# Expert weights in longer rows, some of their lower parts on GpSimd, experts ordered by their count of tokens

## The chip, the core and the metric

One core of a Trainium2 chip runs the whole program. The metric is the device time of one execution in microseconds, lower is better.

## What is computed

The reference is a trunk of two layers. Each has a token mixer (an attention branch and a recurrent branch, merged) and a channel mixer: in the first layer a dense SwiGLU, in the second eight experts of which each token takes two. The change is in the experts alone.

```python
D_MODEL, SEQ, N_EXPERTS, TOP_K, D_FF_EXPERT = 1024, 256, 8, 2, 3584

def swiglu(t, w_gate, w_up, w_down):
    return (jax.nn.silu(t @ w_gate) * (t @ w_up)) @ w_down

def moe_swiglu(h, w_router, b_router, w_gate, w_up, w_down):
    t = h.reshape(B * S, D)
    logits = (t @ w_router).astype(F32) + b_router.astype(F32)
    top_val, top_idx = lax.top_k(logits, TOP_K)
    top_w = jax.nn.softmax(top_val, axis=-1)
    combine = jnp.sum(jax.nn.one_hot(top_idx, N_EXPERTS, dtype=F32) * top_w[..., None], axis=1)
    out = jnp.zeros((B * S, D), F32)
    for e in range(N_EXPERTS):
        out = out + combine[:, e:e + 1] * swiglu(t, w_gate[e], w_up[e], w_down[e]).astype(F32)
    return out.astype(h.dtype).reshape(B, S, D)
```

All data are float32.

## The kernel before

Every product is made of three: each operand is split into an upper part (rounded to the type that TensorE reads at one column a cycle, a copy on ScalarE, L93) and a lower part (the rest, a subtraction on VectorE, L97, by `lower`), and `mm3` (L113 to L115) adds upper x upper, upper x lower and lower x upper in PSUM.

The experts run one after the other, each for 128 slots, whatever its count of tokens; at 128 tokens or fewer the block behind `tc.If` at the end is not entered. `begin` gathers the rows of the first two experts by products with a one-hot matrix (`places_in` builds it, `taken` multiplies, L1271), and makes the first 512 hidden columns of the first expert. `run` then makes a list of parts. A part is 1 MB of weights: four row blocks of 512 columns of gate or up (`column_part`, rows of 2 KB in memory), or two row blocks of whole rows of down (`down_part`, 4 KB). One block of 512 hidden columns is four parts of gate and up, then two parts of down for the block before. `loads` issues the weights on SP's queue into a ring of 14 tiles of 8 KB a partition (`ORDER`, and four tiles once); a tile is free when its lower part is made.

For each part m the emitted order is: its 12 products, hooks of slot 0, the split of the first half of part m + 2 (`half`: ScalarE's copy L93 of 128x1024, then VectorE's L97), hooks of slot 1, the split of the second half, hooks of slot 2. Upper and lower parts have four tiles each (`NSP`), so a half is split when the products of the half four before it are done. Hooks are the small stages: `silu` (L1480, ScalarE from PSUM), `times_up` (L1483, VectorE, one input in PSUM), `turn_hidden` (four transposes, L308), `hidden_high` (L1496, ScalarE) and `hidden_low` (L1500, VectorE from PSUM), `gate_out` (L1504), `gated_high` (L1508) and `gated_low` (L1512, GpSimd), `scatter_in` (L1541) and `scatter_add` (L1545), and for the next pair of experts `places_in` (L1250), `gather_in`, `gather_rows` (L1526), `gather_high` (L1531) and `gather_low` (L1536, GpSimd). Pairs are experts (0,1), (2,3), (4,5), (6,7), gathered in the odd experts. `one_of` makes the second expert's rows of the first pair. The root of the norm is a power on GpSimd (L302).

GpSimd also works at the start of the kernel: `shift_sums` (L544, L548) multiplies and adds tiles there while VectorE splits the first weights (L97, L617).

Of the kernel before, what the change touches and what calls it, by code (L numbers as in the profile page):

```python
# [17 lines left out]
P = 128  # L18
D = 1024
KD = D // P  # L20
S = 256
# [19 lines left out]
def hybrid_trunk_kernel(  # L41
# [12 lines left out]
    pre = pre_stack.enter_context(tc.tile_pool(name="pre", bufs=1, reuse_waits="tile"))   # of the work before the experts  # L54
# [9 lines left out]
    wraw = (wp, "raw", NRAW)  # L64
    ring = [[wraw], 0, []]      # tiles in turn, how many were taken, tiles to take once after the first turn
# [32 lines left out]

    def pairs_of(w):
        return [(w[1][:, j], w[2][:, j]) for j in range(w[1].shape[1])]  # L100

    def piece(src, nk, n):
        """split weights, one (hi, lo) pair for each of the nk row blocks"""
        raw = load_raw(src, nk, n)
        r = []
        for k in range(0, nk, 2):
            w = halves(raw[:, k:k + 2])
            lower(*w)
            r += pairs_of(w)
        return r  # L110
# [7 lines left out]
    side = []      # [generator, steps for each piece, steps owed]  # L118
# [81 lines left out]
    # rows transposed to one column per 128 channels: gains of the four norms, lb rows of both layers, gains of q and k  # L200
    # (1 beyond their 64 channels); the same for b_ada
# [28 lines left out]
    rt = {}      # of the routing  # L230
# [9 lines left out]
    ada = const.tile([P, DEPTH, 4, KD], F32, name="ada")   # sh1, sc1, sh2, sc2 as columns; sc becomes gain*(1+sc)  # L240
# [70 lines left out]
    def affine(tp, dst, l, sc, sh, half):  # L311
        """dst = gain (1 + sc) xn + sh, channels on the partitions"""
# [12 lines left out]
    class HT:  # L325
        """transposed normed activations in two parts, [128 channels, 256 tokens] for each of the 8 channel blocks"""
# [59 lines left out]
    def proj(get, wsrc, col, n, banks=None):  # L386
        """token-major [128, n] PSUM banks of h @ w[:, col:col+n], one for each token tile"""
# [6 lines left out]
    def proj_t(hT, wsrc, col, n):  # L394
        """channel-major: banks of two [128 channels, 256 tokens] blocks of (h @ w[:, col:col+n])^T"""
# [109 lines left out]
    def start(pool, hT, win):  # L505
        """the first weights meet one or two blocks of channels at a time, as their adaLN vectors come in"""
# [24 lines left out]
        def sums(q):  # L531
            """partial sums of the scale over the rows that a partition holds"""
# [8 lines left out]
        def shift_sums(q):  # L541
            """those of the shift, in place"""
# [98 lines left out]
    def mixer(l, hT=None, first=None, half_first=None):  # L641
        with tc.tile_pool(name=f"mix{l}", bufs=1, reuse_waits="tile") as mp:
            win = w_in[l]
            if l:
                # in the order in which their last uses come, the last to be free first
# [16 lines left out]
            # lower bound of the forget gate: none in layer 0, softmax over the layers' rows in layer 1  # L662
# [71 lines left out]
            def hgrn(gi, lfh, lfl, kq, hv):  # L734
# [5 lines left out]
                for hp in range(2):  # L740
# [4 lines left out]
                    for i in range(NT):  # L745
                        e = mp.tile([P, 8, 2, P], F32, tag="ee", bufs=2, name="ee")
                        ee.append(e)
                        # decays to the middle of every block, on all levels, then the keys and queries under them
# [12 lines left out]
                        for li, m in enumerate(LV[:6]):  # L761
                            # keys in the left half of every block, queries in the right half
# [7 lines left out]
                        # pairs of tokens, from their first one on: the decay of the second one, on its query and off its key  # L770
# [6 lines left out]
                        # A^T[s, t]: the pairs of every level, the last of them with the diagonal  # L777
# [42 lines left out]
                # RMS norm over each head  # L820
# [9 lines left out]
            def fox_gate():  # L830
                # transposed: the 16 gate columns (and 16 beyond, unused) stationary, their upper parts beside their lower ones
# [165 lines left out]
    def router_rows(pool, l):  # L997
        """logits = x / rms(x) @ (gain (1 + sc) W) + (sh @ W + b): the weights and the row, before x is there"""
# [10 lines left out]
    def turn_rows(src, dst):  # L1009
        """four 128-channel blocks of x, transposed"""  # L1010
# [12 lines left out]
    def ranks(pool, i):  # L1023
        """the two experts of every token of tile i, as top_k orders them: larger logits first, equal ones by index"""
# [13 lines left out]
    def shares_in(pool):  # L1038
        """softmax over the two logits, in stages: the logits of the two"""
# [25 lines left out]
    def norm(i, hs=None):  # L1065
        """x / rms(x) in two parts"""
# [6 lines left out]
    def place(i, j):  # L1073
        """the places of the tokens of tile i among those of their experts: what the tokens of tile j add"""
# [140 lines left out]
    def moe(l, gate0):  # L1215
        with tc.tile_pool(name="moe", bufs=1, reuse_waits="tile") as mp:
            for tag, n, w in (("s01", 1, 32), ("pv", 1, 32), ("tv", 1, 8), ("ws", 1, 8), ("small", 1, SMALL), ("hid", 2, 512), ("hf", 1, 512), ("g", 3, 2048), ("th", 1, 512), ("tlo", 1, 512), ("ys", 1, 2048),
                              ("raw4", 1, 2048), ("raw8", 1, 2048), ("raw6", 1, 2048), ("raw5", 1, 2048), ("tm", 2, 8), ("ei", 1, 8), ("m8", 1, 8), ("cc", 8, 8), ("raw3", 2, 2048), ("raw2", 1, 2048), ("oneh", 1, 512), ("ohT", 2, 256), ("raw1", 2, 2048), ("raw7", 1, 2048)):
# [18 lines left out]
            # One expert for the slots first .. first+127 of its tokens, in stages: gather, columns of gate and up, rows of  # L1237
            # down, scatter. posc, selc, combc: [128, 1] columns for each token tile.
# [3 lines left out]
            def places_in(pair, i):  # L1242
                oneh = pair[0].get("oneh")
                if oneh is None:
                    oneh = mp.tile([P, NT, 2, P], F32R, tag="oneh", bufs=1, name="oneh")[:, :, :len(pair)]
                for n, ex in enumerate(pair):
                    ex["oneh"] = oneh
                    if ex["first"]:
                        v.tensor_scalar(out=ex["pos"][i], in0=ex["pos"][i], scalar1=float(-ex["first"]), scalar2=None, op0=OP.add)
                    (g if ex.get("e") else v).tensor_scalar(out=oneh[:, i, n], in0=iota, scalar1=ex["pos"][i], scalar2=ex["sel"][i], op0=OP.is_equal, op1=OP.mult)  # L1250
# [14 lines left out]
            def taken(pair, q, i, tp):  # L1265
                """channel blocks 2 q and 2 q + 1 of the tokens of both experts that are in tile i"""
# [39 lines left out]
            def hidden(ex, j):  # L1306
                t = mp.tile([P, 512], F32, tag="hid", bufs=2, name="hid")
# [17 lines left out]
            def gated(ex, h):  # L1325
                yg = mp.tile([P, 512], F32, tag="hid", bufs=2, name="yg")
# [17 lines left out]
            def an_expert(cl, first, w):  # L1344
                return dict(pos=cl[0], sel=cl[1], comb=cl[2], first=first, w=w)

            def begin(pair):
# [3 lines left out]
                xT = mp.tile([P, 512], F32, tag="hid", bufs=2, name="xT")  # L1351
# [30 lines left out]
                room = ["hf", "th", "tlo", "hid"]  # L1382
                hf = [mp.tile([P, 2, P], F32, tag=t, bufs=1 + (t == "hid"), name="hf0") for t in room]
# [41 lines left out]
                one_of(pair, 1, 0, tb[0])  # L1425
                pair[0]["b"] = bk
                pair[0]["tb"] = tb
# [359 lines left out]
```

## Time and profile before

| | |
|---|---|
| median of 3 runs | 1920.51 us (1918.06 to 1923.71) |
| span of the profiled execution | 1922.9 us |
| TensorE busy | 1855.0 us (96%) |
| VectorE busy | 1572.3 us (82%) |
| ScalarE busy | 1309.0 us (68%) |
| GpSimd busy | 212.3 us (11%) |
| read from HBM | 522.72 MB |

The profiled execution has a time of its own, its span; the median is of three executions without a profile. The experts run from about 930 us to the end. Busy time is a sum over stages with different limits, and a matmul's end is modelled: what an engine does in a stage is read from the stretches, the chain and the timeline of that stage.

### The profile page before, as it was taken

Reading aid. Unit: us, or ns where it says so; the run is one execution under the profiler, and the core shown is the slowest. Engines: PE = TensorE matmul, PEld = TensorE weight load, DVE = VectorE, ACT = ScalarE, POOL = GpSimd, SP = SyncE. Lnnn points to the kernel's source line nnn. Section 1 sums busy time; section 2 is a strip of 40 time slices with the busy share of each in tenths; the row PEclk is TensorE's granted clock in tenths of the full one; section 3 lists DMA queues with packets and bytes.
Section 4 is the critical chain, followed back from the end, with each engine's and each line's share of the span. In section 5 each row is a group of like instructions: output and inputs, shape, how many; then the busy total and the mean of one; then the engine's idle time right before and its main releaser. Section 6 shows DMA issues by size and latency. Waiting matters only on the chain.

```text
span 1922.9 us, 25537 instructions
## 1 busy us (share of the span) xinstructions
PE 1855.0 (96%) x9510; PEld 1539.4 (80%) x9510; DVE 1572.3 (82%) x2006; ACT 1309.0 (68%) x1664; POOL 212.3 (11%) x184
## 2 busy tenths in 40 slices
PE   2999999999999999999999999999999999999998
PEld 2787787889987878788787888888888888888887
DVE  6877865878867877447898989999899988999997
ACT  2466558554436665585788787787787878878775
POOL 6701200000000011100000210003100021000000
PEclk9898999999999989999999999999999999999999
DMA  9543653878864525338899999999999999999990
GB/s 300 181 141 110 222 187 118 306 280 308 302 249 134 182 83 174 111 110 306 304 346 355 347 340 370 365 374 343 350 362 362 374 350 340 375 356 368 357 366 26
DMA packets 235140, 525.50 MB, mean 273 GB/s; under 512 B 11756, under 2 KB 23292, under 8 KB 235008
## 3 DMA queue, kind: packets, MB, share of 16 engines
q1 hardware_dynamic: 233624, 523.61, 76.2%
q8 instruction: 76, 1.25, 0.3%
q14 instruction: 56, 0.46, 0.1%
q10 hardware_dynamic: 1384, 0.18, 0.1%
HBM read 522.72 MB, written 1.05 MB: 272 GB/s over the span
## 4 chain that ended last, share of the span: by engine, by line
PE 74%; DVE 2%; ACT 1%; issue 1%; POOL 1%; DVEq 0%; ACTq 0%; POOLq 0%
PE acc L115 15%; PE acc L114 15%; PE acc L113 15%; PE yb L114 5%; PE yb L115 5%; PE yb L113 5%; PE acc L412 2%; PE acc L411 2%; PE acc L413 2%; PE tb L308 2%; DVE wlo L97 1%; PE tb L1541 1%; POOL rs L302 1%; PE tb L798 1%; PE tb L1271 1%
## 5 line engine op out<-in xcount | busy, mean ns | idle before, releaser
L97 DVE TENSOR_TENSOR wlo<-raw,whi 128x1024 fp32r<-128x1024 f32 (+1 forms) x888 | 1077.0, 1237 | 140.6 <-ACT whi L93 123.9
L93 ACT CAST whi<-raw 128x1024 fp32r<-128x1024 f32 (+1 forms) x888 | 919.0, 1047 | 323.6 <-PE acc L115 195.9
L113 PE MATMUL acc<-whi,g 128*128 128x512 f32 x880 | 349.2, 397 | 0.0
L114 PE MATMUL acc<-wlo,g 128*128 128x512 f32 x880 | 344.2, 391 | 0.0
L115 PE MATMUL acc<-whi,g 128*128 128x512 f32 x880 | 344.2, 391 | 0.0
L114 PE MATMUL acc<-wlo,hTh 128*128 128x512 f32 x512 | 209.1, 409 | 6.5 <-DVE wlo L97 6.4
L113 PE MATMUL acc<-whi,hTh 128*128 128x512 f32 x512 | 212.1, 416 | 2.9 <-ACT hTh L615 2.4
L115 PE MATMUL acc<-whi,hTl 128*128 128x512 f32 x512 | 209.9, 410 | 2.6 <-DVE hTl L617 2.6
L114 PEld LDWEIGHTS acc<-wlo,g 128*128 128x128 f32 x880 | 165.5, 188 | 35.8 <-DVE wlo L97 2.8
L115 PEld LDWEIGHTS acc<-whi,g 128*128 128x128 f32 x880 | 165.1, 188 | 35.6
L113 PEld LDWEIGHTS acc<-whi,g 128*128 128x128 f32 x880 | 165.4, 188 | 32.8
L114 PE MATMUL yb<-wlo,th 128*128 128x512 f32 x440 | 172.5, 392 | 4.2 <-DVE wlo L97 4.2
L113 PE MATMUL yb<-whi,th 128*128 128x512 f32 x440 | 171.6, 390 | 0.0
L115 PE MATMUL yb<-whi,tlo 128*128 128x512 f32 x440 | 171.6, 390 | 0.0
L114 PEld LDWEIGHTS acc<-wlo,hTh 128*128 128x128 f32 x512 | 99.2, 194 | 27.8 <-DVE wlo L97 9.9
L115 PEld LDWEIGHTS acc<-whi,hTl 128*128 128x128 f32 x512 | 98.5, 192 | 23.8 <-DVE hTl L617 4.2
L411 PE MATMUL acc<-hTh,whi 128*128 128x256 f32 x416 | 117.2, 282 | 0.0
L412 PE MATMUL acc<-hTl,whi 128*128 128x256 f32 x416 | 116.4, 280 | 0.0
L413 PE MATMUL acc<-hTh,wlo 128*128 128x256 f32 x416 | 116.4, 280 | 0.0
L113 PEld LDWEIGHTS acc<-whi,hTh 128*128 128x128 f32 x512 | 98.2, 192 | 21.9 <-ACT hTh L615 3.1
L302 POOL TENSOR_TENSOR rs<-rs,mhalf 128x8 f32<-128x8 f32 (+1 forms) x28 | 50.9, 1818 | 540.0 <-DVE rs L301 507.8
L114 PEld LDWEIGHTS yb<-wlo,th 128*128 128x128 f32 x440 | 82.6, 188 | 25.9 <-DVE wlo L97 9.3
(382 smaller groups left out, 2645.1 us busy)
## 6 DMA issues: line engine op xcount, KB each, us to landing
raw<-in_moe_w_gate SPq DMA_DIRECT2D x112, 1024.0 KB, 6.0
raw<-in_moe_w_up SPq DMA_DIRECT2D x112, 1024.0 KB, 6.1
raw<-in_moe_w_down SPq DMA_DIRECT2D x110, 1024.0 KB, 5.7
raw<-in_w_in SPq DMA_DIRECT2D x66, 1024.0 KB, 5.1
raw<-in_w_ada SPq DMA_DIRECT2D x48, 1024.0 KB, 6.5
raw<-in_dense_w_gate SPq DMA_DIRECT2D x10, 1024.0 KB, 7.9
raw<-in_dense_w_up SPq DMA_DIRECT2D x10, 1024.0 KB, 7.3
raw<-in_dense_w_down SPq DMA_DIRECT2D x10, 1024.0 KB, 8.6
```

The lines of the kernel that those rows point to most:

```text
L93: a.copy(hi, raw)
L97: v.tensor_sub(lo, raw, hi.bitcast(F32))
L113: pe.matmul(out=o, lhsT=lh, rhs=rh, start=start, stop=False)
L114: pe.matmul(out=o, lhsT=lh, rhs=rl, start=False, stop=False)
L115: pe.matmul(out=o, lhsT=ll, rhs=rh, start=False, stop=stop)
L302: g.tensor_tensor(out=r, in0=r, in1=mhalf[:, :shape[1]], op=OP.pow)
L308: pe.transpose(out=tp[:, b * P:(b + 1) * P], in_=src(b), identity=ident)
L411: pe.matmul(out=o, lhsT=hi, rhs=hT.hh[:, k], start=(k == 0 and c % 2 == 0), stop=False)
L412: pe.matmul(out=o, lhsT=hi, rhs=hT.hl[:, k], start=False, stop=False)
L413: pe.matmul(out=o, lhsT=lo, rhs=hT.hh[:, k], start=False, stop=(k == KD - 1 and c % 2 == 1))
L798: pe.matmul(out=tv[:P - m, li, h, :].rearrange("p (b r) -> p b r", r=m), lhsT=el[:, :P - m], rhs=el.rearrange("p (b s r) -> p b s r", s=2, ...
L1271: pe.matmul(out=tp[:, b * 2 * P:(b * 2 + ne) * P], lhsT=src[:, i, kk * P:(kk + 1) * P], rhs=pair[0]["oneh"][:, i].rearrange("p n t -> p (n ...
```

## The change

- Blocks of hidden columns are 1024 wide (the first expert: 512, then three of 1024; the others: three of 1024, then 512). A part of gate or up is two row blocks of 1024 columns (4 KB rows); a part of down is two neighbouring rows for each partition (8 KB), for which the hidden columns are dealt to the transposes in that order (`PERM`, `view`).
- Of the lower parts, every sixth half (`POOLED`) is subtracted on GpSimd.
- Experts run in an order that is computed: expert 0 first, the others by their rank in the count of tokens (`TURNS`); SP reads the expert's number into a register for the address of its loads. `FEW`, the turns with 64 slots, is empty.
- `begin` gathers one expert; pairs are the turns (1,2), (3,4), (5,6) and the last one alone, gathered in turns 0, 2, 4, 6.
- The ring has 13 tiles instead of 14; `tlo`, `yg` and the tile of the ranking stand in the place of `raw7`.

```diff
+    def lower_pool(raw, hi, lo):
+        g.tensor_sub(lo, raw, hi.bitcast(F32))
...
-("raw1", 2, 2048), ("raw7", 1, 2048)):
+("raw1", 2, 2048),
+                              ("tlo", 1, 1024), ("yg", 1, 512), ("rank", 1, 240)):
...
-                one_of(pair, 1, 0, tb[0])
...
+            def rank_consts():
...
+                for r in range(NE):
+                    g.memset(consts["turn"][:, r:r + 1], float(TURNS[r]))
+                    g.memset(consts["slots"][:, r:r + 1], float(P // 2 if r in FEW else P))
+                    g.memset(consts["few"][:, r:r + 1], float(r in FEW))
             def count():
...
-                v.tensor_reduce(out=cmx, in_=o, axis=AX.X, op=OP.max)
+                v.tensor_copy(consts["cnt"], o)
+                v.tensor_scalar(out=consts["id"], in0=iota[:, :NE], scalar1=0.5, scalar2=float(-4 * S), op0=OP.is_lt, op1=OP.mult)
+                v.tensor_add(consts["rank8"], consts["cnt"], consts["id"])
+            def ranked():
...
+            def turns():
...
+            def by_turn(dst, src):
+                v.tensor_mul(rt["rg"][0], rt["at"], src[:, None, :].to_broadcast([P, NE, NE]))
+                v.tensor_reduce(out=dst, in_=rt["rg"][0], axis=AX.X, op=OP.add)
+            def columns_by_turn(k, src):
+                for i in range(NT):
+                    by_turn(consts[k][:, i], src[:, i])
...
+            def column_part(ex, J, n, q):
+                c0, w_ = ex["blocks"][J]
+                nh, nk = w_ // 512, 2048 // w_
...
+                    for m in range(4):
+                        k, h = nk * q + m // nh, m % nh
...
+                            mm3(o, ex["g"][0][:, k], ex["g"][1][:, k], hi, lo, k == 0, k == KD - 1)
+                def src():
+                    return ex["w"][n].rearrange("(k p) n -> p k n", p=P)[:, nk * q:nk * (q + 1), c0:c0 + w_]
...
+            def down_part(ex, J, q, rows=True):
...
+                    wv = ex["w"][2][c0:c0 + w_].rearrange("(p k) n -> p k n", p=P) if PERM else ex["w"][2][c0:c0 + w_].rearrange("(k p) n -> p k n", p=P)
+                    return wv[:, 2 * q:2 * q + 2] if rows else wv[:, :, 512 * q:512 * (q + 1)]
...
+            def view(ex, J, h):
...
+                if PERM:
+                    m = 512 // nk
+                    return (lambda b: b.rearrange("s (p k) -> s p k", k=nk)), t.rearrange("s (k p) -> s p k", k=nk)[:, m * h:m * (h + 1)]
...
+                def hook_block(ex, J, before, after):
+                    e, w_ = ex["e"], ex["blocks"][J][1]
+                    nh, end = w_ // 512, 2048 // (2048 // w_) // 256 - 1
+                    if e or J:
+                        for h in range(nh):
+                            hook(e, J, "g", end, 1 + h, silu, ex, J, h)
+                            hook(e, J, "u", end, 1 + h, times_up, ex, J, h)
...
+                    for m in range(nb):
+                        k = before[m - nb]
+                        hook(*k, 0, turn_hidden, ex, J, m)
+                        k, sl = ((before[-1], 1), (after, 1))[m]
+                        hook(*k, sl, hidden_high, ex, J, m)
+                        k, sl = ((before[-1], 2), (after, 2))[m]
+                        hook(*k, sl, hidden_low, ex, J, m)
...
+                    if e and J == 1:
+                        for h in range(2):
+                            hook(e, 1, "g", 2 * h, 1, gate_out, exs[e - 1], h)
+                            hook(e, 1, "g", 2 * h, 2, gated_high, exs[e - 1], h)
+                            hook(e, 1, "g", 2 * h + 1, 1, gated_low, exs[e - 1], h)
...
+                for q, f, *args in ((1, count), (2, ranked), (3, turns)):
+                    hook(0, 1, "g", q, 2, f, *args)
+                for q, k, src in ((0, "pos", pos), (0, "sel", sel)):
+                    hook(0, 1, "u", q, 0, columns_by_turn, k, src)
...
+                hook(0, 3, "u", 1, 1, columns_by_turn, "comb", comb)
...
+                hook(e, last, "g", end, 0, silu, ex, last, 0)
+                hook(e, last, "g", end, 0, silu_few, ex, last)
...
+                        e = parts[m]["key"][0]
+                        if e == len(known):
+                            r = nc.values_load(consts["idi"][0:1, e:e + 1], engines=(mybir.EngineType.SP,), min_val=0, max_val=NE - 1)
...
                 def half(m, k):
                     if m < len(parts):
                         w = halves(raws[m][:, k:k + 2])
-                        lower(*w)
+                        nlow[0] += 1
+                        (lower_pool if POOLED and nlow[0] % POOLED == 0 else lower)(*w)
...
-ORDER = "72385w614"
+ORDER = "2385w614"
...
+TURNS = (0, 1, 4, 5, 2, 6, 7, 3)
+FEW = ()
+PERM = True
+POOLED = 6
```

## Rows read from the trace of the kernel before

**Rows 1.** The page, busy time: engine, us, share of the span, instructions.
```profile
PE 1855.0 (96%) x9510; PEld 1539.4 (80%) x9510; DVE 1572.3 (82%) x2006; ACT 1309.0 (68%) x1664; POOL 212.3 (11%) x184
```
**Rows 2.** Stretches of two experts: length, busy by engine, clock, DMA share, GB/s.
```profile
1328.41:1453.48 125.07, 124.58 (x576) 102.50 (x575) 112.66 (x106) 100.22 (x117) 15.71 (x10) 1.00 0.98 353
1453.48:1574.52 121.04, 120.57 (x544) 98.89 (x543) 112.62 (x105) 95.32 (x101) 11.51 (x6) 1.00 1.00 365
```
**Rows 3.** Chain that ended last: start, us, the transposes of single blocks.
```profile
1243.07 0.44 PE tb L308 x4
1259.88 0.44 PE tb L308 x4
...
1328.41 0.44 PE tb L308 x4
...
1453.48 0.44 PE tb L308 x4
```
**Rows 4.** Groups by form, 1000 to 1850 us: count, busy, mean ns, idle before.
```profile
L97 DVE TENSOR_TENSOR wlo<-raw,whi 128x1024 fp32r<-128x1024 f32 x581 | 704.1, 1241 | 71.6 <-ACT whi L93 58.0 <-PE acc L115 3.9
L93 ACT CAST whi<-raw 128x1024 fp32r<-128x1024 f32 x581 | 605.1, 1052 | 138.7 <-PE acc L115 79.5 <-PE yb L115 48.2 <-DVE wlo L97 8.9
...
L1500 DVE TENSOR_TENSOR tlo<-tb,th 128x512 fp32r<-128x512 f32 x48 | 32.8, 682 | 0.0
L1483 DVE TENSOR_TENSOR hid<-hid,acc 128x512 f32<-128x512 f32 x48 | 32.6, 678 | 0.0
L1480 ACT ACTIVATE hid<-acc 128x512 f32<-128x512 f32 x49 | 29.1, 593 | 0.0
```
**Rows 5.** Timeline of the experts: start, us, engine, instruction, count, idle before.
```profile
1099.49 5.82 DVE L97 TENSOR_TENSOR wlo<-raw,whi 128x1024 fp32r<-128x1024 f32 x5
...
1076.78 1.56 POOL L1512 TENSOR_TENSOR ys<-yg,ys 128x512 fp32r<-128x512 f32 x1 [4.69 <-ACT ys L1508]
...
1077.69 1.73 DVE L97 TENSOR_TENSOR wlo<-raw,whi 128x1024 fp32r<-128x1024 f32 x1 [0.51 <-ACT whi L93]
...
1079.48 0.50 PE L114 MATMUL yb<-wlo,th 128*128 128x512 f32 x1 [0.49 <-DVE wlo L97]
```
**Rows 6.** Timeline at the start of the kernel, GpSimd, then VectorE.
```profile
26.18 3.60 POOL L544 TENSOR_TENSOR raw<-raw,cact 128x2048 f32<-128x2048 f32 x1 [2.52 <-DMA raw<-in_w_ada]
29.86 3.21 POOL L548 TENSOR_TENSOR raw<-raw 128x1024 f32<-128x1024 f32 x1
53.52 2.14 POOL L548 TENSOR_TENSOR raw<-raw 128x512 f32<-128x512 f32 x1
...
26.33 4.53 DVE L97 TENSOR_TENSOR wlo<-raw,whi 128x1024 fp32r<-128x1024 f32 x1
30.78 2.83 DVE L617 TENSOR_TENSOR hTl<-hf,hTh 128x512 fp32r<-128x512 f32 x1
...
54.45 0.15 DVE L563 TENSOR_TENSOR ada<-tb,bcol 128x2 f32<-128x2 f32 x1
```
**Rows 7.** Waits of SP's queue (us in total, times, longest); the page's DMA issues.
```profile
SPq L86 <- DVE wlo L97: 1295.1, 402, 23.7
...
raw<-in_moe_w_gate SPq DMA_DIRECT2D x112, 1024.0 KB, 6.0
```
**Rows 8.** First expert: chain, stretch, GpSimd and VectorE timeline, gather, fills.
```profile
929.31 3.61 PE acc L1271 x16
...
929.30:932.70 3.40, 3.39 (x16) 3.40 (x17) 2.36 (x5) 1.74 (x5) 0.00 (x0) 0.53 1.05 408
...
923.33 0.55 POOL L302 TENSOR_TENSOR rs<-rs,mhalf 128x1 f32<-128x1 f32 x1 [10.47 <-DVE rs L301]
...
917.34 0.22 DVE L1034 TENSOR_TENSOR rg<-rg,rg 128x64 f32<-128x64 f32 x1
...
1088.73 0.94 PE tb L1271 x8
...
L866 POOL MEMSET ka<- 128x16 f32 x4 | 0.5, 128 | 88.0 <-DVE sg L715 70.6 <-PE tb L817 17.4
```

More of the change, by code (lines that the diff above doesn't have):

```diff
@@ L1464, in down_part @@
-            def down_part(ex, j, h, rows=True):
+                        ex.setdefault("b", [None, None])[n] = [acc_bank() for _ in range(nh)]
+                    for m in range(4):
+                        k, h = nk * q + m // nh, m % nh
+                        o, (hi, lo) = ex["b"][n][h], w[m]
+                        if ex["few"]:
+                            pe.matmul(out=o, lhsT=ex["g"][:, k], rhs=hi, start=(k == 0), stop=False)
+                            pe.matmul(out=o, lhsT=ex["g"][:, k], rhs=lo, start=False, stop=(k == KD - 1))
+                        else:
+                            mm3(o, ex["g"][0][:, k], ex["g"][1][:, k], hi, lo, k == 0, k == KD - 1)
@@ L1490, in hidden_high @@
[L1490 to L1500 removed]
+                    hid = ex["h"][J]
@@ new lines, in products @@
+                    for m in range(4):
+                        k, c = (2 * q + m // 2, m % 2) if rows else (m, q)
+                        first, last = J == 0 and k == 0, J == len(ex["blocks"]) - 1 and k == nk - 1
+                        o, (hi, lo) = ex["y"][c], w[m]
+                        if ex["few"]:
+                            pe.matmul(out=o, lhsT=hid[0][:, k], rhs=hi, start=first, stop=False)
+                            pe.matmul(out=o, lhsT=hid[0][:, k], rhs=lo, start=False, stop=last)
+                        else:
+                            mm3(o, hid[0][:, k], hid[1][:, k], hi, lo, first, last)
@@ new lines, in silu, with silu_few @@
+            def silu(ex, J, h):
+                if h == 0:
+                    ex["t"] = mp.tile([P, 1024], F32, tag="hid", bufs=1, name="hid")
+                f, t = view(ex, J, h)
+                b = ex["b"][0][h]
+                if not ex["few"]:
+                    a.activation(out=t, in_=f(b), func=AF.Silu)
+                    return
+                a.copy(t, f(b[P // 2:]))
+                v.tensor_add(t, t, f(b[:P // 2]))
+            def silu_few(ex, J):
+                t = ex["t"][:P // 2, :ex["blocks"][J][1]]
+                a.activation(out=t, in_=t, func=AF.Silu)
@@ new lines, in times_up, with turn_hidden @@
+            def times_up(ex, J, h):
+                f, t = view(ex, J, h)
+                b = ex["b"][1][h]
+                if not ex["few"]:
+                    v.tensor_mul(t, t, f(b))
+                    return
+                u = mp.tile([P, 512], F32, tag=("yg", "hf")[h], bufs=1, name="ug")[:P // 2]
+                a.copy(u, b[P // 2:])
+                v.tensor_add(u, u, b[:P // 2])
+                v.tensor_mul(t, t, f(u))
+            def turn_hidden(ex, J, m):
+                t = ex["t"]
+                if ex["few"]:
+                    nk, n = ex["blocks"][J][1] // P, P // 2
+                    tp = t_bank()
+                    for k in range(nk):
+                        pe.transpose(out=tp[:, k * n:(k + 1) * n], in_=t[:n, k * P:(k + 1) * P], identity=ident[:n, :n])
+                    ex["tv", 0] = tp[:, :nk * n].rearrange("p (k t) -> p k t", k=nk)
+                else:
+                    ex["tv", m] = transpose4(lambda b: t[:, (4 * m + b) * P:(4 * m + b + 1) * P])[1]
@@ new lines, in hidden_high @@
+            def hidden_high(ex, J, m):
+                nk = ex["blocks"][J][1] // P
+                if m == 0:
+                    if ex["e"] == NE - 1 and J == len(ex["blocks"]) - 1:
+                        t = mp.tile([P, 2, 8, P], F32R, tag="g", bufs=3, name="g")
+                        ex["h"][J] = [t[:, 0, :nk]] if ex["few"] else [t[:, n, :nk] for n in range(2)]
+                    elif ex["few"]:
+                        t = mp.tile([P, 8, P], F32R, tag="th", bufs=1, name="th")
+                        ex.setdefault("h", {})[J] = [t[:, :nk]]
+                    else:
+                        ex.setdefault("h", {})[J] = [mp.tile([P, 8, P], F32R, tag=n, bufs=1, name=n)[:, :nk] for n in ("th", "tlo")]
+                hid = ex["h"][J]
+                if ex["few"]:
+                    a.copy(hid[0][:, :, :P // 2], ex["tv", 0])
+                else:
+                    a.copy(hid[0][:, 4 * m:4 * m + 4], ex["tv", m])
@@ L1570, in run, with hook @@
             def run(exs):
-                last = NJ - 1
                 parts, hooks = [], {}
-                def hook(key, slot, f, *args):
-                    hooks.setdefault((key, slot), []).append((f, args))
+                def hook(s, J, kind, q, slot, f, *args):
+                    hooks.setdefault(((s, J, kind, q), slot), []).append((f, args))
                 def hooked(key, slot):
@@ new lines, in run @@
+                hook(0, 3, "u", 1, 1, columns_by_turn, "comb", comb)
+                ex = exs[-1]
+                last = len(ex["blocks"]) - 1
+                parts += [down_part(ex, last, h, False) for h in range(2)]
+                e, w_ = ex["e"], ex["blocks"][last][1]
+                end = w_ // 256 - 1
+                hook(e, last, "g", end, 0, silu, ex, last, 0)
+                hook(e, last, "g", end, 0, silu_few, ex, last)
+                hook(e, last, "u", end, 0, times_up, ex, last, 0)
@@ L1723, in moe @@
                             scatter(ex, h)
+                    for i in range(NT):
+                        v.tensor_scalar(out=pos[:, i], in0=pos[:, i], scalar1=float(-P), scalar2=None, op0=OP.add)
                     for h in range(2):
```

280 lines of the change are left out of this document (142 added, 138 removed).

## The prediction, made before the change was run

> **What bounds the kernel now.** I read the page first: over the whole span TensorE is busy 1855.0 of 1922.9 us, VectorE 1572.3, GpSimd only 212.3 [rows 1]. An average says little, so next come the stretches of one expert each, cut where the chain of work that ended last shows the same transposes: an expert in which the next pair's rows are gathered takes 125.07 us, one without 121.04 [rows 2, 3]. In them TensorE is busy 124.58 and 120.57, at the full clock (1.00). One block of 512 hidden columns takes 1259.88 - 1243.07 = 16.81 us [rows 3]; it holds 72 matmuls and 4 transposes (0.44), so (16.81 - 0.44) / 72 = 0.227 us a matmul. So the experts (about 980 us of the span) are bound by matmuls, and the change leaves their number alone: `FEW` is empty, so all experts keep 128 slots and three products.
>
> The second look goes to VectorE, which is the next engine: busy 112.66 and 112.62 us of those stretches, so idle 12.4 and 8.4 us, 10.4 on the mean [rows 2]. Nearly all is the lower part of the weights (L97): 581 of them against 48 of each hook [rows 4]. Back to back, five take 5.82 us, so one occupies (5.82 - 1.24) / 4 = 1.15 us [rows 4, 5]. The third look goes to the loads: SP waited 1295.1 us for L97 to free a tile, and a load lands 6.0 us after its issue [rows 7], so the stream stands a full ring ahead (14 tiles of 16.81 / 6 = 2.8 us, 39 us) and does not limit anything.
>
> **What can be won** is therefore small. TensorE's own waits in one such expert are one of about 0.5 us: GpSimd's L1512 starts at 1076.78, VectorE's L97 beside it takes 1.73 instead of 1.24 us, and TensorE waits for it at 1079.48 [rows 5]. Seven of these are under 5 us.
>
> **The change part by part.**
>
> *Loads.* Gate and up come in 4 KB rows, down in 8 KB ones. The queue waits for tiles, not the tiles for the queue [rows 7]: gain nil. The ring loses one tile of 14, leaving 13 x 2.8 = 36 us of lead against 6.0 us of landing: cost nil. From the second expert on, SP loads a register with the expert's number before it issues; behind it on SP stand only later loads. The trace shows no such load; the nearest row of this queue is a landing, 6.0 us, beside 36 us of lead, so I take nil; with the lead gone it would be up to 6.0 us for each of seven experts, 42 us, and never a gain.
>
> By the Trainium skill (DMA: Bandwidth & Descriptors, Where 436 GB/s comes from) a core's HBM share of about 358 GB/s would bind such a stream; here 365 GB/s are moved over an expert while SP still waits for free tiles [rows 2, 7], so the measurement decides and no term comes of it.
>
> *Lower parts on GpSimd.* Every sixth half goes from L97 to `lower_pool`, which is 14 of an expert's 84. What that costs VectorE is read at the start of the kernel, where GpSimd does the same kind of work, two SBUF inputs, 128x1024. GpSimd's L544 runs from 26.18 to 29.78; VectorE's L97, begun at 26.33, ends at 30.86, that is 1.08 us after GpSimd's end. GpSimd's L548 on 128x1024, begun at 29.86, ends at 33.07, which is 2.21 us after VectorE's end, and VectorE's next, begun at 30.78, ends 0.54 us after that [rows 6]. So the two take strict turns: whoever runs holds the other for all of it, 2.21 us for GpSimd and 1.08 for VectorE. An operation with an input in PSUM is not held: L563 took 0.15 us at 54.45 while GpSimd ran from 53.52 to 55.66 [rows 6].
>
> So a half that moves takes 1.15 us off VectorE and puts a hold of 2.21 us in its place: 14 x (2.21 - 1.15) = +14.8 us an expert in the chain that VectorE and GpSimd now form. Cover within it: operations from PSUM that stand right behind a moved half. By the order of the hooks these are `hidden_low` at the last down part of three blocks and `gate_out` of one half, four of 0.68 us [rows 4], or 0.6 without the overlap that L97 shows (1.24 against 1.15): 2.4 us. The rest must come out of VectorE's idle time, 10.4 us: 14.8 - 2.4 - 10.4 = +2.0 us an expert. Not all idle time can be used, since in gathering experts VectorE waits behind ScalarE, which waits for TensorE's gather (the 4.0 us between 12.4 and 8.4); of that I count half as lost, 1.0 us on the mean of both kinds. That makes +3.0 us an expert, times 7.9 experts' worth of parts (332 / 42) = +24 us. Ends: nothing, if more of the holds falls beside operations from PSUM than the order shows; and +7.2 us an expert (57 us in all) if only half the idle time can be used. I take the value near the lower end because VectorE may lag some 2 us before TensorE notices: a half is started three halves (4.1 us) ahead of its use and needs 1.05 + 1.15 us [rows 4, 5].
>
> The Trainium skill has a rule that speaks against this step (SBUF — State Buffer, Who interferes with whom): GpSimd and a VectorE instruction with two SBUF inputs share a port pair as an exclusive lock, held for the whole instruction, not as a split of bandwidth. By it each moved half would cost the whole instruction; by the rows it is 2.21 us after the other has let go, and the trace agrees, so the sum stays.
>
> *Latency of a moved half.* ScalarE 1.05, GpSimd 2.21, some 0.2 to start: 3.5 us of the 4.1 + 0.2 at which TensorE reads it (the upper part is read one matmul earlier). It fits with 0.8 us to spare; with VectorE's operation in front (1.08) it does not. This is where the waits of the chain will show.
>
> *Blocks of 1024 columns.* As many ScalarE, VectorE and transpose instructions as before (two of each per block instead of one per 512). ScalarE's `hidden_high` now stands between the two splits of a part and waits for the last down products, as the split behind it does anyway: nil, at most its own 0.6 us for each block. One place is tighter: in the first block of experts 2 to 7 only two down parts lie behind the last up part, and the transposes now stand after the first of them instead of the second. `times_up` of the second half comes four VectorE operations behind (two L97, two of 0.60), about 4.7 us after the middle of the up part; TensorE is there at 1.36 + 2.73 = 4.1 us: 0.6 us, six times, 4 us. Where the chain above binds, this wait is part of it; it is added only in the first rival. The permuted views of the hidden rows write with a stride; no row shows that, so from 0 to doubling L1480's and L1483's 0.6 us; I take 0, as the element counts are the same.
>
> *First expert and gathers.* Only one expert is gathered in `begin`: 16 products of 256 columns took 3.61 us at a granted clock of 0.53 (1.2 of 2.4 GHz) [rows 8] and are halved, -1.8, but VectorE's first rows then come late by about half of that: -1. The eighth expert is gathered alone in the seventh: four times half of 0.94 [rows 8], +2. `one_of` goes, which I count at nothing. The ranking adds some 28 small operations of 0.22 us on VectorE [rows 8], 6 us, within the first expert, where idle time is taken already: +3, ends 0 and +6. Its 24 fills on GpSimd (0.13 each, 3 us) stand ahead of the root at L302, which waits 10.47 us there [rows 8]: nil, and +3 if that cover is gone.
>
> *End.* One extra Silu for 64 slots lies under four down parts (11 us): nil.
>
> **Sum** against the profiled execution: 1922.9 + 24 - 1 + 2 + 3 = 1951 us. Its span is 2.4 above the median of the three runs (1920.5), so the forecast is 1948 us.
>
> **The rivals.**
> 1. *Covered: not slower.* The holds fall into VectorE's idle time and beside its operations from PSUM. It decides as soon as the usable cover reaches 14.8 us an expert; counted, there are 12.8, and the 0.07 us that a waiting L97 saves 14 times (1.15 - 1.08) add 1.0, so 1 us more is enough. For it: the margin is thin. Against it: chains that are full to the last per cent wait somewhere, as the single hold of rows 5 already does. Time: 1920.5 - 5 (waits of rows 5) + 4 (tight transposes) + 1 = 1921, from 1915 to 1926.
> 2. *Faster.* The stream or its landing limits after all, or L1512's wait is gone and no new one comes: -5 and more, 1908 to 1914. Against it are rows 7 and TensorE's 0.227 us.
> 3. *Late halves everywhere.* If half the idle time or less can be used, or TensorE's clock falls when it waits (it was granted 0.53 after the waits in `begin` [rows 8]), the cost passes 57 us: 1980 and up.
> 4. *Nothing done.* The order by count changes no work at 128 slots; that part alone is a difference of zero, and is counted in the first rival.
>
> **How the numbers follow.** Forecast (the chain of VectorE and GpSimd binds, +6 to +60): 0.65; covered: 0.21; faster: 0.06; late everywhere: 0.08. The likeliest gives 1948. The range goes from 1914 (bottom of covered) to 1983 (half the idle time used, 57 + 4 above 1922.9 less 2.4, rounded up). A measurement tells 0.3%, 6 us, from no change: faster 0.06, same 0.21, slower 0.73.
>
> **What would show it.** In the changed profile: `lower_pool` of 2.2 to 3.3 us each, L97 beside it up to 3.3 us; VectorE's share in an expert near 100% with GpSimd's holds in it; TensorE waiting for GpSimd's and VectorE's lower parts, a few us an expert, and stretches of an expert of about 126 us. Right rival 1: the stretches stay at 121 to 125. Loads: SP still waits for tiles, ScalarE never for a load. Wrong altogether: ScalarE waiting for DMA, or the matmuls' 0.227 us changed.

## The result

The changed kernel takes **2031.49 us** (median of four runs, 2026.38 to 2032.76); the kernel before, beside it, takes 1919.28 (1915.44 to 1923.71). The ratio is 1.058, interval 1.056 to 1.060: **112 us slower**, where the forecast was 28 us slower and the range ended at 1983. The profiled execution has a span of 2029.9 us.

Four parts of the page after (busy time; TensorE's clock in 40 slices; groups as line, engine, shapes, count, busy, mean ns, idle before), which answer to [rows 1, 4]:

```profile
PE 1897.7 (93%) x9542; PEld 1549.3 (76%) x9542; DVE 1592.4 (78%) x1918; ACT 1328.3 (65%) x1665; POOL 513.8 (25%) x324
PEclk9999999999999999998999999999999999999999
L97 DVE TENSOR_TENSOR wlo<-raw,whi 128x1024 fp32r<-128x1024 f32 (+1 forms) x778 | 1066.0, 1399 | 231.2 <-ACT whi L93 229.2
L100 POOL TENSOR_TENSOR wlo<-raw,whi 128x1024 fp32r<-128x1024 f32 x110 | 284.4, 2585 | 664.5 <-ACT whi L93 409.1
L117 PE MATMUL yb<-wlo,th 128*128 128x512 f32 x440 | 184.2, 419 | 38.9 <-DVE wlo L97 31.4
```

110 lower parts went to GpSimd, 2.59 us each on the mean. The largest of TensorE's waits on this page, 38.9 us, stand at one kind of product, those of down parts that read a lower part of the weights. TensorE's busy time has grown by 43 us with 32 more matmuls of some 9,500. The slices of its clock, 51 us each, show nearly full speed; the short slow stretches that are found below don't come out in them.

The stretches of two turns (length, busy by engine, clock, DMA share, GB/s), an odd one that gathers nothing and an even one that gathers for the next two, which answer to [rows 2]:

```profile
1096.00:1227.60 131.60, 124.73 (x545) 99.62 (x544) 113.12 (x91) 97.49 (x102) 39.57 (x16) 0.99 0.94 342
1227.60:1367.30 139.70, 129.43 (x576) 102.96 (x575) 115.18 (x91) 102.75 (x118) 62.16 (x28) 0.99 0.87 311
```

An expert takes 131 to 140 us in place of 121 and 125. And VectorE is **not** full: 113 of 131.6 us, 86%, and 115 of 139.7, 82%, with the time in which it is held counted as busy. The prediction's own sign, a share near 100%, did not come. TensorE waits for lower parts while the engine that makes them has 18 us to spare. So it is not a sum of busy times that ran over, as the prediction had it, but single halves that come late. One such place, an odd turn, timeline of TensorE, VectorE and GpSimd (start, us, instruction, count, idle before):

```profile
1438.78 0.51 PE L117 MATMUL yb<-wlo,th 128*128 128x512 f32 x1 [1.75 <-DVE wlo L97]
...
1432.46 1.08 DVE L1568 TENSOR_TENSOR hid<-hid,acc 128x512 f32<-128x512 f32 x1
1433.45 1.21 DVE L97 TENSOR_TENSOR wlo<-raw,whi 128x1024 fp32r<-128x1024 f32 x1
1434.58 1.09 DVE L1568 TENSOR_TENSOR hid<-hid,acc 128x512 f32<-128x512 f32 x1
1435.58 0.74 DVE L1664 SCALAR_TENSOR_TENSOR xt<-tb,rank,xt 128x512 f32<-128x512 f32 x1
1436.23 3.63 DVE L97 TENSOR_TENSOR wlo<-raw,whi 128x1024 fp32r<-128x1024 f32 x2
...
1435.25 2.40 POOL L100 TENSOR_TENSOR wlo<-raw,whi 128x1024 fp32r<-128x1024 f32 x1 [6.07 <-ACT whi L93]
```

Between 1432.46 and 1437.65, the end of GpSimd's operation, VectorE finishes one lower part. First come the two `times_up` of the block, 1.08 us each where it was 0.68 [rows 4]; then GpSimd starts at 1435.25, and the L97 begun at 1436.23 stands still until GpSimd ends at 1437.65. TensorE needs a half every 1.36 us and is some three halves behind its start. Steps of over 2 us from one matmul to the next come 27 times in the experts; before, none did there.

The experiments use the same cut everywhere: from the end of one expert's last down product to the next. In this table "plain" is a turn without a gather and "gather" one that gathers for two, each the mean of two such turns.

| kernel | plain | gather | time | ratio, interval |
|---|---|---|---|---|
| before | 121.1 | 125.1 | | 1 |
| changed | 133.2 | 140.1 | 2031.5 | 1.058, 1.056 to 1.060 |
| e1: nothing on GpSimd | 123.3 | 130.6 | 1957.6 | 1.021, 1.019 to 1.023 |
| e2: no strides | 126.7 | 134.9 | 1993.4 | 1.040, 1.038 to 1.042 |
| e3: neither | 121.2 | 127.1 | 1935.8 | 1.009, 1.007 to 1.011 |
| e4: before, with GpSimd | 122.4 | 130.0 | 1941.7 | 1.012, 1.010 to 1.014 |
| e5: late transposes | 128.5 | 137.2 | 2010.8 | 1.049, 1.047 to 1.051 |
| e6: every twelfth | 125.5 | 133.5 | 1976.1 | 1.030, 1.028 to 1.032 |
| e7: e2, placed | 123.9 | 138.8 | 1984.8 | 1.035, 1.033 to 1.037 |
| e8: e2, spread | 123.1 | 134.9 | 1977.4 | 1.030, 1.028 to 1.032 |
| e9: e3, gather_low first | 121.2 | 127.1 | 1932.5 | 1.006, 1.005 to 1.008 |
| e10: e8, odd turns only | 122.9 | 127.2 | 1941.6 | 1.011, 1.009 to 1.013 |
| e11: e9, three turns of 64 slots | | | 1925.4 | 1.003, 1.002 to 1.005 |
| e12: e3, gather_rows later | 121.2 | 125.6 | 1931.0 | 1.006, 1.004 to 1.008 |

### The profile page after: what moved, and what is told of

It reads as the page before. It is cut to its first block, busy times and chain, and to the rows that moved or that the text cites. A ratio compares the mean times of both kernels' runs of the same rounds, so it can differ in the third digit from the quotient of the medians.

```text
span 2029.9 us, 26375 instructions
## 1 busy us (share of the span) xinstructions
PE 1897.7 (93%) x9542; PEld 1549.3 (76%) x9542; DVE 1592.4 (78%) x1918; ACT 1328.3 (65%) x1665; POOL 513.8 (25%) x324
## 5 line engine op out<-in xcount | busy, mean ns | idle before, releaser
L97 DVE TENSOR_TENSOR wlo<-raw,whi 128x1024 fp32r<-128x1024 f32 (+1 forms) x778 | 1066.0, 1399 | 231.2 <-ACT whi L93 229.2
L100 POOL TENSOR_TENSOR wlo<-raw,whi 128x1024 fp32r<-128x1024 f32 x110 | 284.4, 2585 | 664.5 <-ACT whi L93 409.1
L117 PE MATMUL acc<-wlo,g 128*128 128x512 f32 x880 | 348.9, 397 | 15.1 <-DVE wlo L97 9.6
L117 PE MATMUL yb<-wlo,th 128*128 128x512 f32 x440 | 184.2, 419 | 38.9 <-DVE wlo L97 31.4
L116 PE MATMUL yb<-whi,th 128*128 128x512 f32 x440 | 180.8, 411 | 0.0
L118 PE MATMUL yb<-whi,tlo 128*128 128x512 f32 x440 | 180.0, 409 | 0.0
```

The source lines that it names most:

```text
L97: v.tensor_sub(lo, raw, hi.bitcast(F32))
L100: g.tensor_sub(lo, raw, hi.bitcast(F32))
L116: pe.matmul(out=o, lhsT=lh, rhs=rh, start=start, stop=False)
L117: pe.matmul(out=o, lhsT=lh, rhs=rl, start=False, stop=False)
L118: pe.matmul(out=o, lhsT=ll, rhs=rh, start=False, stop=stop)
```

## The experiments

### One part taken back, the other, both; and one part alone

**e1**, nothing on GpSimd:

```diff
-POOLED = 6
+POOLED = 0
```

> The changed kernel with all lower parts on VectorE (POOLED 0), all else as changed. Theory G (GpSimd's holds cause most of the loss): the first products of down parts that wait over 1 us (26 in the experts, 54 us), the waits for lower_pool at gate and up (14 to 22 us) and most of the half-clock stretches (19 us) go, so 1930 to 1950 us, and the lower parts are back at 1.24 us each. Theory S (the strided views of the hidden rows, silu and times_up at 1.1 instead of 0.6 to 0.68 us, cause most of it): 1990 us or more. The prediction's own account, 24 us for the holds: 2007 us.

**e2**, no strides:

```diff
-PERM = True
+PERM = False
```

> The changed kernel with the down rows in blocks (PERM off): down parts in 4 KB rows and the hidden rows read and written without a stride; GpSimd keeps every sixth lower part. silu and times_up back at 0.60 and 0.68 us. Theory S: 1950 us or less. Theory G: only the waits of the transposes in the first blocks shrink (6 x 0.8) and a few us of the others, 2010 to 2025 us. The prediction counted the strides at nothing: 2031 us.

**e3**, both edits.

> The changed kernel with both undone: all lower parts on VectorE and the hidden rows without a stride; what stays are the blocks of 1024, the order by count, one expert gathered at first and the ring of 13. If the two act apart, the gains of the first two add up; if both only feed the same lateness of VectorE, either alone gets most of it. Prediction's account without its holds: 1924 us. If the blocks of 1024 cost by themselves (the transposes behind the first of two down parts, 6 x 0.5 to 2.5 us): up to 1940 us.

**e4**, in the kernel before:

```diff
-                        lower(*w)
+                        nlow[0] += 1
+                        (lower_pool if nlow[0] % 6 == 0 else lower)(*w)
```

> The kernel before with every sixth lower part on GpSimd and nothing else changed. The prediction: +24 us, 1944 us, range 1920 to 1977. Theory G: +70 us or more, 1990 us and up. Theory S: under +30 us, for without the strides VectorE has the room that the prediction counted.

Measured: 1957.6, 1993.4, 1935.8 and 1941.7 us. Neither theory holds alone. From e3 up, the strides cost **22 us** (e1), the moved parts **58 us** (e2), and what stays of the change **17 us** over the kernel before. These make 96; the other 16 appear only where both are on. `PERM` also sets the rows of the down parts, 8 KB or 4 KB, but SP waits for free tiles either way (718.0 us from 1000 to 1900 us in e1, 698.3 in e3), so the loads are not what costs the 22 us. In the kernel before, the moved parts cost **22.8 us** (e4); the prediction had 24.

The strides are seen in single operations. VectorE's groups by form, 1000 to 1900 us, in the changed kernel and then in e2:

```profile
L1568 DVE TENSOR_TENSOR hid<-hid,acc 128x512 f32<-128x512 f32 x46 | 49.5, 1076 | 0.0
```
```profile
L1568 DVE TENSOR_TENSOR hid<-hid,acc 128x512 f32<-128x512 f32 x48 | 32.4, 675 | 0.0
```

and ScalarE's `silu` in the same two:

```profile
L1555 ACT ACTIVATE hid<-acc 128x512 f32<-128x512 f32 x46 | 51.0, 1108 | 1.8 <-PE acc L118 1.8
```
```profile
L1555 ACT ACTIVATE hid<-acc 128x512 f32<-128x512 f32 x48 | 28.5, 594 | 1.8 <-PE acc L118 1.8
```

Same elements, same bytes: 1.6 and 1.9 times as long when the view steps by 128 elements. By the Trainium skill (Advanced Engine Details and Errata, SBUF Cachelines) an access pattern needs two hits in each 16-byte line of SBUF to run at full speed and pays where each access opens a new one; these views do that, and the trace agrees.

Where the GpSimd cost lies in e4 is seen in its stretches, gather and plain, and in the first product of down on its page:

```profile
1061.40:1191.40 130.00, 126.55 (x577) 102.06 (x576) 113.35 (x91) 100.40 (x117) 59.66 (x28) 1.00 0.96 340
1191.40:1313.80 122.40, 120.98 (x545) 98.82 (x544) 108.11 (x91) 95.30 (x101) 38.90 (x17) 1.00 1.00 361
...
L117 PE MATMUL yb<-wlo,th 128*128 128x512 f32 x440 | 175.3, 399 | 13.8 <-POOL wlo L100 9.4
```

+1.3 us in a plain turn, +5.0 in one that gathers. Here too VectorE is only 87 to 88% busy, with the same number of moved parts, 110, as in the changed kernel and in e2.

### Where the waits sit

**e5**, the transposes one part later where only two down parts lie behind a block:

```diff
-                        k = before[m - nb]
+                        k = before[m - nb] if len(before) > 2 else (before[-1], after)[m]
                         hook(*k, 0, turn_hidden, ex, J, m)
```

> The changed kernel; where only two down parts lie behind a block of 1024, the first four transposes come after the second down part and the other four after the first part of the next columns, one part later than now. If the transposes are a wait of their own (2.5 us, six times, and half-clock stretches behind some): 2010 to 2016 us. If VectorE's lateness behind GpSimd sets the end and the transposes are only where it shows: 2025 us or more, with the first products of down waiting longer in exchange.

2010.8 us: 20.7 less, so these six waits were mostly their own; if VectorE's lateness alone had set the end, the waits would have come back elsewhere. One of them in the changed kernel, TensorE, VectorE, GpSimd:

```profile
1222.58 0.93 PE L311 MATMUL tb<-ident,hid 128*128 128x128 f32 x4 [2.30 <-DVE hid L1568]
...
1217.26 2.23 DVE L97 TENSOR_TENSOR wlo<-raw,whi 128x1024 fp32r<-128x1024 f32 x1 [1.12 <-ACT whi L93]
1219.41 1.06 DVE L1568 TENSOR_TENSOR hid<-hid,acc 128x512 f32<-128x512 f32 x1
1220.38 1.21 DVE L97 TENSOR_TENSOR wlo<-raw,whi 128x1024 fp32r<-128x1024 f32 x1
1221.52 1.01 DVE L1568 TENSOR_TENSOR hid<-hid,acc 128x512 f32<-128x512 f32 x1
...
1216.00 2.40 POOL L100 TENSOR_TENSOR wlo<-raw,whi 128x1024 fp32r<-128x1024 f32 x1 [5.50 <-ACT whi L93]
```

The first L97 stands still until GpSimd ends at 1218.40 and is done at 1219.49; two long `times_up` follow with an L97 between them, and the transposes read the second. In e1, without the hold, this step (matmul start to matmul start) is 1.75 us instead of 2.71; in e2 and e3, without the strides, it is under 0.6.

What follows such a wait is the second half of the price. TensorE's clock (the column 1.00, 0.50, 1.00) in the wait, in the next 3.4 us and after:

```profile
1219.87:1222.80 2.93, 0.63 (x4) 0.23 (x3) 2.93 (x4) 1.15 (x2) 0.00 (x0) 1.00 1.00 369
1222.80:1226.20 3.40, 3.40 (x11) 2.81 (x10) 1.99 (x2) 0.10 (x1) 0.00 (x0) 0.50 0.96 345
1226.20:1229.60 3.40, 3.40 (x18) 2.76 (x17) 1.83 (x2) 2.64 (x4) 0.53 (x1) 1.00 0.94 363
```

The granted clock is 1.2 of 2.4 GHz for 3.4 us, which costs half of them, 1.7 us. The changed kernel has 12 such stretches in the experts, each at the end of a step of over 2 us or within 2 us behind it (12 of the 27 such steps have one). e2 has three, e1 and e3 one each, and e5, without the six waits of the transposes, four. Those 9 more than the two single parts explain, at up to 1.7 us, are up to 15 us: most of the 16 that appear only where both are on. TensorE's idle time bears this out: from the end of `begin` to the last few us it is 71.7 us as changed, 52.8 in e2, 25.9 in e1 and 11.4 in e3, so only some 4 of the 16 are more waiting, and the rest is longer busy time. No run changed the clock alone, so this is read, not tried. Nearest to a trial is the first turn, where the wait of 2.6 us for the ranking (see below) has a slow stretch behind it in e3 and none in e10: the turn takes 142.0 and 140.2 us, though e10 spreads its `times_up` as well.

**e6**, half as many moved parts:

```diff
-POOLED = 6
+POOLED = 12
```

> The changed kernel with every twelfth instead of every sixth lower part on GpSimd (7 of 84 an expert). At 0, 14 per expert the runs gave 1958 and 2031 us. If each hold costs alike: 1994 us. If it matters where a hold falls, theory B (a hold costs most where it stands right behind the two times_up of a block of 1024, which come within three halves of weights): by the order of the parts, those holds (second half of the third down part) are not among the seven from the third expert on, so 1975 us or less.

1976.1 us: the first seven of an expert cost 18.5 us, the other seven 55. The cost does not go by number alone; the bound of theory B, 1975, was missed by 1 us. By itself this could also be a cover that seven parts leave unused and fourteen use up. e4, e7 and e8 keep the number at 14 and change the place.

**e7** and **e8** start from e2. e7 places the parts, e8 spreads the two `times_up`:

```diff
+                        e, J, kind, q = parts[m]["key"]
+                        late = k and ((kind, q) in (("d", 3), ("g", 3), ("u", 3)) or exs[e]["blocks"][J][1] == 512 and (kind, q) in (("g", 0), ("u", 0)) or exs[e]["blocks"][J][1] == 1024 and (kind, q) == ("u", 1))
+                        (lower_pool if late else lower)(*w)
```
```diff
-                            hook(e, J, "u", end, 1 + h, times_up, ex, J, h)
+                            k, sl = ((e, J, "u", end), 1) if h == 0 else (before[0], 1)
+                            hook(*k, sl, times_up, ex, J, h)
```

> The changed kernel without strides (PERM off, which gave 1993 us; with nothing on GpSimd 1936), and still 14 lower parts an expert on GpSimd, but placed by their part: none from one part before the two times_up of a block to two parts behind them (second halves of the fourth gate part, the second and the fourth up part and the fourth down part; in the block of 512 of the first gate and up parts). Theory B: a hold costs what it costs in the kernel before, +23 for all, so 1960 us or less. If holds cost by their number: 1993 us.

> The changed kernel without strides (PERM off, 1993 us), every sixth lower part on GpSimd as there, but the second times_up of a block one part later, behind the first down part. Theory B (bunching): the waits of 2.1 us at the first products of down (two in an expert) shrink to about 1 us as in the kernel before with GpSimd's parts, 1965 to 1978 us. If the hold alone is the price: 1990 to 1995 us.

1984.8 and 1977.4 us: e7 misses its bound of 1960 by 25 us, e8 is at the upper end of its range. Theory B holds in plain turns: 126.7 falls to 123.9 and 123.1, and the steps of 2.1 us are gone there in e8. It misses in turns that gather: 134.9 stays in e8 and becomes 138.8 in e7. Two places show why. The longest wait of e7, on GpSimd:

```profile
1228.90 2.51 POOL L100 TENSOR_TENSOR wlo<-raw,whi 128x1024 fp32r<-128x1024 f32 x1 [0.82 <-ACT whi L93]
1231.40 5.70 POOL L1256 TENSOR_SCALAR oneh<-iota,rank 128x128 fp32r<-128x128 f32 x2
1237.08 3.08 POOL L100 TENSOR_TENSOR wlo<-raw,whi 128x1024 fp32r<-128x1024 f32 x1
```

Two one-hot rows of `places_in` hold GpSimd for 5.7 us, and the moved part behind them is done at 1240.16; TensorE's step in front of it is 3.4 us. GpSimd's queue has work of its own, and the moved parts wait in it.

The other place stands in e2 and, at nearly the same times, in e8. ScalarE, GpSimd and VectorE in e2:

```profile
1309.90 1.02 ACT L1638 ACTIVATE hf<-tb,ada 128x256 f32<-128x256 f32 x2 [2.01 <-POOL g L1655]
...
1311.99 2.36 POOL L100 TENSOR_TENSOR wlo<-raw,whi 128x1024 fp32r<-128x1024 f32 x1 [2.12 <-issue]
...
1312.83 2.60 DVE L97 TENSOR_TENSOR wlo<-raw,whi 128x1024 fp32r<-128x1024 f32 x1 [3.56 <-ACT whi L93]
```

ScalarE waits 2.0 us for `gather_low`, as it does without moved parts (e3, below); the splits stand behind it and VectorE is idle for 3.6 us. Then a moved half is next: GpSimd has it done at 1314.35, and the L97 beside it stands still until then. TensorE's step, which ends at 1314.40, is 2.4 us here and 1.2 at the same place in e3.

**e10**, e8 with parts moved in odd turns only:

```diff
-(lower_pool if POOLED and nlow[0] % POOLED == 0 else lower)(*w)
+(lower_pool if POOLED and nlow[0] % POOLED == 0 and parts[m]["key"][0] % 2 else lower)(*w)
```

> The changed kernel without strides and with the second times_up spread (1977 us, 41 us above the same with nothing on GpSimd), but lower parts go to GpSimd only in the odd turns, which gather nothing. Theory Q: in the turns that gather, moved parts stand on GpSimd behind its own work (one-hot rows of 2.4 to 2.9 us, gather_low of 1.6) and that work behind them, so nearly all of the 41 us is there; the odd turns cost 1.9 us each and the time is 1942 to 1948 us. If holds cost alike in all turns: 1956 us.

1941.6 us, 0.4 under the range that theory Q gave, and 5.7 over e3. So of e8's 41 us over e3 the odd turns hold some 6 (122.9 us each against 121.2); the other 35 lie in the turns that gather, the first one among them.

### What stays without the two

e3's 17 us lie in turns that gather (127.1 against 125.1, and 124.9 in turn 6, which gathers for one, against 121.1) and in the first turn. In a turn that gathers, e3 shows ScalarE, GpSimd, VectorE and TensorE thus:

```profile
1287.49 1.02 ACT L1638 ACTIVATE hf<-tb,ada 128x256 f32<-128x256 f32 x2 [2.01 <-POOL g L1655]
...
1284.30 3.16 POOL L1655 TENSOR_TENSOR g<-hf,g 128x256 fp32r<-128x256 f32 x2 [20.59 <-ACT g L1646]
...
1289.48 2.36 DVE L97 TENSOR_TENSOR wlo<-raw,whi 128x1024 fp32r<-128x1024 f32 x2 [2.62 <-ACT whi L93]
...
1290.76 0.51 PE L117 MATMUL yb<-wlo,th 128*128 128x512 f32 x1 [0.76 <-DVE wlo L97]
```

`gather_rows` of the fourth quarter waits for `gather_low` of the third, which still reads their one tile; the splits of the weights stand behind it on ScalarE.

Both from e3: **e9**, `gather_low` emitted earlier; **e12**, `gather_rows` of the next quarter later:

```diff
-(2, ("g", 1, 0), ("g", 1, 1), ("g", 1, 2), ("u", 0, 1))
+(2, ("g", 1, 0), ("g", 1, 1), ("g", 1, 2), ("g", 1, 2))
```
```diff
-(3, ("u", 0, 0), ("u", 0, 1), ("u", 1, 1), ("u", 1, 2))
+(3, ("u", 0, 0), ("u", 1, 1), ("u", 1, 2), ("u", 1, 2))
```

> The changed kernel with nothing on GpSimd and no strides (1936 us), and gather_low of the third quarter right behind its gather_high instead of two parts later. Its turns that gather take 127.1 us against 121.2 for the others (before: 125.05 and 121.06). Theory Q: part of the 2 us more is that ScalarE's gather_rows of the fourth quarter waits 2.0 us for GpSimd's gather_low of the third, which still reads the tile, with the upper parts of the weights queued behind it; then the gathering turns fall to 125.5 to 126 us and the time to 1930 us. If that wait is covered: 1936 us.

> The changed kernel with nothing on GpSimd and no strides (1936 us); gather_rows of the fourth quarter one part later (with the second up part of the block of 512 in place of the first), its gather_high and gather_low right behind it. GpSimd was idle before the gather_low that ScalarE waits for, so emitting that one earlier could not move it; moving the one who waits can. Theory Q: ScalarE's wait of 2.0 us for GpSimd goes, TensorE's two waits behind it (1.2 and 0.6 us) shrink, and the turns that gather for two fall from 127.1 to 126 us or less: 1929 to 1932 us. If those waits do not set the length of these turns: 127 us and 1936 us.

e9 left the turns at 127.1 us, and the wait of 2.0 us stood in its trace as before: GpSimd had been idle for 20 us, so an earlier place in the program moved nothing. Its 1932.5 us is not told apart from 1935.8 by that. e12 took the wait away; the turn fell to 125.6 and the time to 1931.0, which by itself would not be told apart from e9's: the turns show it.

The first turn is 10.6 us longer than the first expert of before (same products, from the end of `begin`); 5.9 are its gather, and the 4.7 left are put down to the ranking, which no run took out. In e3 VectorE runs 18 small operations in a row, and TensorE stands behind them, with a slow stretch of 3.4 us after it:

```profile
953.74 0.22 DVE L1473 TENSOR_TENSOR rank<-rank 128x64 f32<-128x64 f32 x1
...
957.54 0.22 DVE L1484 TENSOR_REDUCE rank<-rg 128x8 f32<-128x64 f32 x1
957.68 2.40 DVE L97 TENSOR_TENSOR wlo<-raw,whi 128x1024 fp32r<-128x1024 f32 x2
...
959.00 0.50 PE L117 MATMUL acc<-wlo,g 128*128 128x512 f32 x1 [2.26 <-DVE wlo L97]
```

**e11**, e9 with the change's own provision for small counts, two products instead of three:

```diff
-FEW = ()
+FEW = (1, 4, 7)
```

> As the first of these, with three turns (1, 4, 7: the smallest counts) at 64 slots, two products in place of three; nothing on GpSimd. TensorE then has some 38 us less to do in each of the three. If VectorE's lower parts set the end there (112.6 us busy in an expert before, and some 7 us more for its sums of half banks): 1910 to 1932 us. If TensorE still did: 1820 us.

1925.4 us, 7 under e9 though TensorE has 38 us less to do in each of three turns. The first of them:

```profile
1073.20:1192.40 119.20, 103.19 (x413) 70.27 (x413) 112.98 (x111) 95.30 (x106) 3.10 (x2) 0.99 0.98 365
```

VectorE is busy 113 of 119.2 us there (95%); the lower parts set the end. The loads do not: SP waits 92 of these us for L97 to free tiles, and no engine waits for a load. No version run here is faster than the kernel before.

## Why the prediction was wrong

The sign was right, the size was not: the sum had +28 and the runs show +112. By its own steps:

- **Lower parts on GpSimd, +24: the step that failed.** In the changed order they cost 58 us alone. In the kernel before it is 22.8 (e4), but that the number fits there is luck: the prediction filled VectorE's idle time with holds until it was full, and VectorE is never full (82 to 88%), in e4 as in the changed kernel. What counts is the lead of about three halves at the place where a hold falls. The prediction had this in its paragraph on the latency of a moved half (it fits with 0.8 us to spare, with a VectorE operation in front it does not), but gave it no term: it balanced the holds against the idle time of a whole expert and did not ask what stands beside each in the new order. There both `times_up` of a block come within three halves, and the moved parts meet the gathers' own work in GpSimd's queue: e8, e10 and e7 show the two places. That gathering turns cost more was said, as 1.0 us on the mean, and is 5.0 against 1.3 in e4.
- **Permuted views, "from 0 to doubling, I take 0".** They nearly double, and cost 22 us alone. The upper end was in the text and did not reach the range; equal element counts were the wrong reason.
- **The tight transposes, 0.6 us six times, in the first rival only.** 2.5 us six times as changed, 1.5 with the strides alone, nothing seen without strides: the strides make the wait, the holds lengthen it, and e5 got 20.7 us by moving the transposes.
- **TensorE's clock.** Named in the third rival (chance 0.08), left out of the sum. Its 12 stretches cost up to 20 us (half of 3.4 us each). The outcome is that rival's 1980 and up, but by late halves, the strides and the clock, not by a lack of idle time.
- **First turn and gathers, +4 in all.** Measured +17 (e3): the ranking 4.7 (3 predicted, within its ends), the lone gather 3.8 (2), `begin` 1.1 longer (1 shorter was predicted), and an unseen 2 us in each of three turns, of which e12 gave back 1.5 by moving the stage that waits for the one tile of two quarters. These make 15 to 16 of the 17. The hooks of the gathers were read as moved, not as put closer together.
- **Right:** the loads cost and gain nothing. SP waits 1123.7 us for L97 and 230.2 for L100 to free tiles (below), and plain turns of e3 and e12 run at 121.2. A moved half takes 2.35 to 3.36 us, 2.42 in the median, where 2.2 to 3.3 were told, and L97 beside it stands still.

```profile
SPq L86 <- DVE wlo L97: 1123.7, 402, 23.6
SPq L86 <- POOL wlo L100: 230.2, 88, 5.0
```

## What to carry to other kernels

When work moves to an engine that can hold another, don't compare sums of busy time: take the lead in time at each place where a hold falls, and add what else stands in those few microseconds in the *new* order, on both queues. A view with a large stride is priced at its upper bound until a row shows otherwise. A long wait of TensorE may have to be charged for the slow stretch behind it as well.

## What the runs showed of the hardware

- fp32 operations with a step of 128 elements in SBUF took 1.08 instead of 0.68 us on VectorE and 1.11 instead of 0.59 on ScalarE (128x512, one operand in PSUM).
- The granted clock fell to 0.50 for 3.4 us at 12 of 27 steps of over 2 us; e4, whose waits in the experts are about 1 us, shows no such stretch there. The length of one wait does not tell it alone: e12 has a step of 2.6 us without a stretch, and e11 has stretches behind steps of 1.4 to 1.7 us.
- A VectorE subtraction of two SBUF inputs that met one on GpSimd stood still until that one had ended, and was done 1.09 us after it (1218.40 and 1219.49 above).
